# One split per pair of gate tiles, ordered a block ahead, and a shorter TensorE part of the sample sum

## The chip, the cores and the metric

The kernel runs on one core of one Trainium2 chip. Its time is the device time of that core in microseconds (us), taken as the median of several runs. The profile is one further execution, recorded by the hardware profiler; its engines are named PE (TensorE matmul), PEld (TensorE weight load), DVE (VectorE), ACT (ScalarE), POOL (GpSimd) and SP (SyncE, which issues most DMAs).

## The reference, cut to what matters

The model step has two layers, each a mixer (an RG-LRU in layer 0, a convolution in layer 1) followed by a PEER channel mixer. The change lies in the channel mixer alone. For every token it scores 2 x 128 keys per head, keeps 16 experts of 16,384 for each of 8 heads, and sums over them:

```python
top_s, pos = lax.top_k(cand, TOPK)
expert = jnp.take_along_axis(cand_idx, pos, axis=-1)
g = jax.nn.softmax(top_s, axis=-1)
u = u_tab[expert]
v = v_tab[expert]
act = jax.nn.gelu(jnp.einsum('td,thkd->thk', xb, u))
return jnp.einsum('thk,thkd->td', g * act, v)
```

There are 256 prompt tokens and 32 sample tokens. Both tables are 16,384 x 1024 in float32.

## The kernel before, in words

**Dense columns.** For 240 of the 256 prompt tokens nothing is gathered: the kernel computes the product with every expert. The tables are cut into 128 pieces of 128 experts each. Piece j of the first table gives a "u block": 24 matmuls (8 slices of the model dimension, each in three parts of a split product) into the tile `pu`, then a gelu by ACT into column j of `store`. A "gate phase" for each of three groups of pieces (0 to 45, 46 to 93, 94 to 127) multiplies `store` by the gates of the chosen experts: DVE builds one-hot tiles (`oA`, `oB`), PE multiplies them (`pgt`), DVE multiplies `store` by the result. Piece j of the second table gives a "v block": 24 matmuls (L1317 to L1319) that add to four accumulators `acc`.

**Split products.** A float32 matrix is split in two fp32r parts: ACT rounds it (the high part), DVE subtracts to get the low part, and three matmuls stand for one product. Each table tile `raw` is so split into `wh` (L234, ACT) and `wl` (L235, DVE), two blocks ahead of its use, into three buffers each. Columns j and j+1 of `store` are split together, as a pair, into `gh` (L439, ACT) and `gl` (L440, DVE), with two buffers each; `gw` holds which halves stand ready for which block. This is done by `wsplit(j)`, which does nothing if `gw` has j, or if the gate phase of j's group is still in the list `bg`.

**When a pair is split before the change.** An even block j calls `wsplit(j)`. After the block, `gw.pop(j)` removes only its own half. The odd block j+1 then calls `wsplit(j)` again: since the half of j has gone, the whole pair is split a second time into the other buffers, and block j+1 uses the halves of this second split. It then calls `wsplit(j + 2)` for the next pair. So there are two `gh` and two `gl` instructions a pair, both in front of the odd block.

**Order of blocks.** 82 u blocks come first, then two v blocks and two u blocks by turns until the u blocks end, then the remaining v blocks (the last two after the loop). Each engine executes its instructions in the order in which the program wrote them.

**The planner.** Beside the blocks runs background work on DVE: the gate phases (list `bg`), and the chain `bg2`. The latter holds the work for the 16 prompt tokens outside the dense columns (`extra`) and for the 32 sample tokens (`sample`). Both gather table rows by indirect DMAs from POOL into `grow` (L1369), multiply and sum on DVE. After each block, `pump` compares two estimates, `tp` for PE and `td` for DVE, and writes background steps into the program while `td` is lower. A `wsplit` that does something adds 620 to `td`.

**The sample sum.** The last part of `sample` adds 32 gathered rows of the second table, weighted by `act`. Its first `CPS[l]` steps are matmuls (`so`, L1485) that a copy by ACT brings to `sacc`; the others are DVE instructions into `sacd` (L1480 and L1478), one after each block. Each step orders the gather of the row two steps later.

Of the kernel before, what the change touches and what calls it, by code (L numbers as in the profile page):

```python
# [95 lines left out]
BG2 = (3, 0)  # L96
BG3 = (32, 32)
BG4 = 1
CPS = (14, 14)
J1 = 46  # L100
J2 = 94
CHUNKS = [(0, J1), (J1, J2), (J2, 128)]
# [99 lines left out]
class Stream:  # L202
# [39 lines left out]
    def next(self, src, idx, look=2):  # L242
        i = self.use_n
        self.use_n += 1
        assert self.items[i][0] is src and self.items[i][1] == idx, (i, self.items[i][1], idx)
        while self.split_n <= min(i + look, len(self.items) - 1):
            self._split()
        return self.hl.pop(i)


def peer_order():
    order = [("u", j) for j in range(RING)]
    u, v = RING, 0
    while v < 128:
        order += [("v", v), ("v", v + 1)]
        v += 2
        if u < 128:
            order += [("u", u), ("u", u + 1)]
            u += 2
    return order  # L260


class Kern:
# [867 lines left out]
    def peer(self, l):  # L1131
# [159 lines left out]
        gw = {}  # L1291

        def wsplit(j):
            c = [i for i, (j0, j1) in enumerate(CHUNKS) if j0 <= j < j1]
            if j in gw or not c or G[c[0]] in self.bg:
                return
            wh = wp.tile([128, 2, ND], F32R, name="gh", tag="gh", bufs=2)
            wl = wp.tile([128, 2, ND], F32R, name="gl", tag="gl", bufs=2)
            self.split_act(wh, wl, store[:, j % RING:j % RING + 2])
            self.td += 620  # L1300
            for i in range(2):
                gw[j + i] = (wh[:, i], wl[:, i])
# [8 lines left out]
        def vmm(j, w, d):  # L1311
            wh, wl = gw[j]
            vh, vl = w
            o = acc[d // 2][:, d % 2, :ND]
            f = j == 0 and d % 2 == 0
            e = j == 127 and d % 2 == 1
            nc.tensor.matmul(o, vh[:, d], wh, start=f, stop=False, skip_group_check=True)  # L1317
            nc.tensor.matmul(o, vh[:, d], wl, start=False, stop=False, skip_group_check=True)  # L1318
            nc.tensor.matmul(o, vl[:, d], wh, start=False, stop=e, skip_group_check=True)  # L1319

        for kind, j in peer_order():
            if kind == "v":
                if l == 0 and j in ADJ:
                    next(self.fg)
                for c, (j0, j1) in enumerate(CHUNKS):
                    if j == j0:
                        self.flush(G[c])
                wsplit(j - j % 2)
                if j % 2:
                    wsplit(j + 1)  # L1330
            if j >= 126 and kind == "v":
                continue
            w = self.wnext()
            if kind == "u":
                if j % 2 == 0:
                    pu = ps.tile([128, 2, NP], F32, name="pu", tag="mm", bufs=2)
                self.mm3(pu[:, j % 2, :ND], w, [(k, k) for k in range(KT)], aH, aL, 0, ND, True, True)
                if j % 2:
                    s = j % RING - 1
                    nc.scalar.activation(store[:, s:s + 2], pu[:, :, :ND], AF.Gelu)  # L1340
                done["u"] = self.udone = j + j % 2
                self.td += 1200
            else:
                if acc is None:
                    self.von = True
                    acc = [ps.tile([128, 2, NP], F32, name=f"acc{i}", tag="acc", bufs=4) for i in range(4)]
                for d in range(KT):
                    vmm(j, w, d)
                gw.pop(j)
                self.td += 1200  # L1350
            self.tp += 2690
            self.pump()
# [72 lines left out]
    def sample(self, l, TKs):  # L1425
# [15 lines left out]
        rows = {}  # L1441
        CP = CPS[l]
        gather = self.gatherer(ei, rows)
# [116 lines left out]
```

## Time and profile before

| | |
|---|---|
| median of 3 runs | 2409.42 us (2404.04 to 2414.55) |
| profiled execution | 2391.81 us, its span 2390.0 us |
| PE busy | 2100.3 us, 88% of the span |
| DVE busy | 1751.8 us, 73% |
| ACT busy | 977.2 us, 41% |
| POOL busy | 294.5 us, 12% |
| mean granted TensorE clock | 0.951 of full speed |
| DMA | 493.92 MB, mean 207 GB/s |

The u and v blocks of layer 0 lie between 258 and 1175 us, those of layer 1 between 1426 and 2360 us. A group of instructions reads: line, engine, operation, output and inputs, shape, count | busy time, mean ns of one | idle time of the engine just before them, and what ended it. A row of the table by stretches reads: stretch in us, its length, then busy time (and number of instructions) of each engine, the granted TensorE clock, the busy share of the DMA engines, and GB/s. In a timeline the columns are the start, the duration, the instruction, and in brackets the idle time before it and what ended it.

### The profile page before, as it was taken

Reading aid. Unit: us, or ns where it says so; the run is one execution under the profiler, and the core shown is the slowest. Engines: PE = TensorE matmul, PEld = TensorE weight load, DVE = VectorE, ACT = ScalarE, POOL = GpSimd, SP = SyncE. Lnnn points to the kernel's source line nnn. Section 1 sums busy time; section 2 is a strip of 40 time slices with the busy share of each in tenths; the row PEclk is TensorE's granted clock in tenths of the full one; section 3 lists DMA queues with packets and bytes.
Section 4 is the critical chain, followed back from the end, with each engine's and each line's share of the span. In section 5 each row is a group of like instructions: output and inputs, shape, how many; then the busy total and the mean of one; then the engine's idle time right before and its main releaser. Section 6 shows DMA issues by size and latency. Waiting matters only on the chain. (4 is left out here: it accounts for less than half of the span.)

```text
span 2390.0 us, 46892 instructions
## 1 busy us (share of the span) xinstructions
PE 2100.3 (88%) x19234; PEld 1944.3 (81%) x19234; DVE 1751.8 (73%) x3502; ACT 977.2 (41%) x1341; POOL 294.5 (12%) x329
## 2 busy tenths in 40 slices
PE   7999999988888888887888889999988888788877
PEld 3788999988888877776876689999888888778776
DVE  3877998887677766674776779898876777666666
ACT  1845444444333333343342544444443433333333
POOL 1100003030000000033112000120300000000330
PEclk9999999999999988998999999999998999899999
DMA  9774468576566544487579545685855666444873
GB/s 363 259 284 132 157 187 301 172 264 210 176 195 195 186 142 152 150 318 263 205 196 295 197 136 167 194 292 170 293 181 170 198 198 194 124 115 144 297 260 132
DMA packets 135912, 493.92 MB, mean 207 GB/s; under 512 B 16032, under 2 KB 16544, under 8 KB 135056
## 3 DMA queue, kind: packets, MB, share of 16 engines
q1 hardware_dynamic: 93168, 334.09, 43.3%
q0 software_dynamic: 42528, 156.83, 19.6%
q8 instruction: 151, 2.47, 0.4%
q14 instruction: 65, 0.53, 0.1%
HBM read 483.41 MB, written 7.39 MB: 205 GB/s over the span
## 5 line engine op out<-in xcount | busy, mean ns | idle before, releaser
L235 DVE TENSOR_TENSOR wl<-raw,wh 128x1024 fp32r<-128x1024 f32 x583 | 707.6, 1220 | 390.8 <-ACT wh L234 355.2
L234 ACT CAST wh<-raw 128x1024 fp32r<-128x1024 f32 x583 | 609.1, 1046 | 693.7 <-PE acc L1318 461.3
L1318 PE MATMUL acc<-gl,wh 128*128 128x240 f32 x2048 | 615.9, 301 | 200.9 <-DVE gl L440 200.6
L1318 PEld LDWEIGHTS acc<-gl,wh 128*128 128x128 f32 x2048 | 428.4, 209 | 223.6 <-DVE gl L440 223.6
L1317 PE MATMUL acc<-gh,wh 128*128 128x240 f32 x2048 | 606.0, 296 | 2.3 <-ACT gh L439 2.3
L1319 PE MATMUL acc<-gh,wl 128*128 128x240 f32 x2048 | 602.2, 294 | 0.0
L465 PE MATMUL pu<-aH,wl 128*128 128x240 f32 x2048 | 565.6, 276 | 9.2 <-DVE wl L235 9.1
L463 PE MATMUL pu<-aH,wh 128*128 128x240 f32 x2048 | 567.7, 277 | 0.0
L464 PE MATMUL pu<-aL,wh 128*128 128x240 f32 x2048 | 564.2, 276 | 0.0
L1317 PEld LDWEIGHTS acc<-gh,wh 128*128 128x128 f32 x2048 | 427.5, 209 | 18.1 <-issue 10.1
L1319 PEld LDWEIGHTS acc<-gh,wl 128*128 128x128 f32 x2048 | 429.0, 209 | 0.0
L465 PEld LDWEIGHTS pu<-aH,wl 128*128 128x128 f32 x2048 | 390.4, 191 | 11.5 <-DVE wl L235 11.5
L463 PEld LDWEIGHTS pu<-aH,wh 128*128 128x128 f32 x2048 | 389.0, 190 | 1.2 <-issue 0.8
L464 PEld LDWEIGHTS pu<-aL,wh 128*128 128x128 f32 x2048 | 389.5, 190 | 0.0
L439 ACT CAST gh<-store 128x480 fp32r<-128x480 f32 x254 | 150.3, 592 | 166.0 <-PE acc L1319 165.8
L440 DVE TENSOR_TENSOR gl<-store,gh 128x480 fp32r<-128x480 f32 x254 | 157.3, 651 | 23.5 <-ACT gh L439 23.4
L1340 ACT ACTIVATE store<-pu 128x480 f32<-128x480 f32 x128 | 73.1, 571 | 227.0 <-PE pu L465 226.9
L1369 POOL DMA_INDIRECT grow<-ur,ei x64 | 63.6, 994 | 752.2 <-DVE grow L1452 620.1
L463 PE MATMUL prj<-aH,wh 128*128 128x288 f32 x392 | 118.8, 303 | 0.0
L1282 DVE SCALAR_TENSOR_TENSOR store<-pgt,store 128x460 f32<-128x460 f32 (+3 forms) x184 | 83.8, 499 | 46.5 <-PE pgt L1275 46.1
L1251 DVE TENSOR_TENSOR oA<-c,iT 128x1280 f16<-128x1280 f16 (+1 forms) x136 | 116.4, 856 | 0.0
L464 PE MATMUL prj<-aL,wh 128*128 128x288 f32 x392 | 115.7, 295 | 0.0
(366 smaller groups left out, 2688.4 us busy)
## 6 DMA issues: line engine op xcount, KB each, us to landing
raw<-ut SPq DMA_DIRECT2D x256, 512.0 KB, 4.0
raw<-vt SPq DMA_DIRECT2D x256, 512.0 KB, 3.9
adaw<-wada POOLq DMA_DIRECT2D x56, 512.0 KB, 8.6
raw<-w SPq DMA_DIRECT2D x54, 512.0 KB, 5.4
raw<-wq SPq DMA_DIRECT2D x32, 512.0 KB, 3.6
adaw<-wada SPq DMA_DIRECT2D x18, 512.0 KB, 6.2
R<-us POOLq DMA_DIRECT2D x32, 286.5 KB, 10.0
store<-wada POOLq DMA_DIRECT2D x12, 512.0 KB, 4.2
```

Source lines behind the costliest of these rows:

```text
L234: nc.scalar.copy(hf, r)
L235: nc.vector.tensor_sub(lf, r, hf.bitcast(F32))
L439: self.nc.scalar.copy(h, src)
L440: self.nc.vector.tensor_sub(lo, src, h.bitcast(F32))
L463: nc.tensor.matmul(pt, h[:, kb], ah[:, ka, n0:n1], start=f, stop=False)
L464: nc.tensor.matmul(pt, h[:, kb], al[:, ka, n0:n1], start=False, stop=False)
L465: nc.tensor.matmul(pt, lo[:, kb], ah[:, ka, n0:n1], start=False, stop=e)
L1251: v.tensor_tensor(a, self.iota2[:, None].to_broadcast([128, g, 128, 2]), bc(0, 128), op=ALU.is_equal)
L1282: v.scalar_tensor_tensor(sv, pg[:, :n, q0 - j0:q1 - j0].rearrange("p t j -> p j t"), 1.0 / 4096.0, sv, op0=ALU.mult, op1=ALU.mult)
L1317: nc.tensor.matmul(o, vh[:, d], wh, start=f, stop=False, skip_group_check=True)
L1318: nc.tensor.matmul(o, vh[:, d], wl, start=False, stop=False, skip_group_check=True)
L1319: nc.tensor.matmul(o, vl[:, d], wh, start=False, stop=e, skip_group_check=True)
```

## The change

The two halves of a pair stay in `gw` until the odd block has used them, so that the pair is split once; the split of the next pair is ordered behind the matmuls of the even block, not in front of the odd block. `CPS` goes from (14, 14) to (8, 4): in layer 0 the first 8 and in layer 1 the first 4 steps of the sample sum are matmuls, the other 24 and 28 are DVE instructions. The number of dense columns stays at 240.

```diff
-CPS = (14, 14)
+CPS = (8, 4)
...
                 for d in range(KT):
                     vmm(j, w, d)
-                gw.pop(j)
+                if j % 2:
+                    del gw[j - 1], gw[j]
+                else:
+                    wsplit(j + 2)
                 self.td += 1200
             self.tp += 2690
             self.pump()
```

The lines behind L1349 move down by three (L1478 becomes L1481, L1485 becomes L1488).

On DVE, near the end of layer 1, where v blocks run alone and each is followed by one step of the sample sum, this stands in a row before (numbers tell buffers apart; `wl` belongs to a v block two blocks later):

```order
L1478 SCALAR_TENSOR_TENSOR sacd_26294<-grow_26521,sact_21230,sacd_26294 128x1024
L440 TENSOR_TENSOR gl_26599<-store_15315,gh_26598 128x480
L440 TENSOR_TENSOR gl_26603<-store_15315,gh_26602 128x480
L235 TENSOR_TENSOR wl_26609<-raw_26491,wh_26608 128x1024
L1478 SCALAR_TENSOR_TENSOR sacd_26294<-grow_26562,sact_21230,sacd_26294 128x1024
L235 TENSOR_TENSOR wl_26642<-raw_26532,wh_26641 128x1024
L1478 SCALAR_TENSOR_TENSOR sacd_26294<-grow_26595,sact_21230,sacd_26294 128x1024
```

and this with the change:

```order
L1481 SCALAR_TENSOR_TENSOR sacd_24956<-grow_25484,sact_20952,sacd_24956 128x1024
L235 TENSOR_TENSOR wl_25560<-raw_25454,wh_25559 128x1024
L440 TENSOR_TENSOR gl_25588<-store_15057,gh_25587 128x480
L1481 SCALAR_TENSOR_TENSOR sacd_24956<-grow_25521,sact_20952,sacd_24956 128x1024
L235 TENSOR_TENSOR wl_25597<-raw_25487,wh_25596 128x1024
L1481 SCALAR_TENSOR_TENSOR sacd_24956<-grow_25554,sact_20952,sacd_24956 128x1024
L235 TENSOR_TENSOR wl_25630<-raw_25524,wh_25629 128x1024
```

One `gl` a pair is left of two, and it stands behind the `wl` of the same even block and in front of that block's background step. Of the two `gl` before, the first is the second split of the pair in use.

On ACT, around the copy that ends the TensorE part of the sample sum in layer 1, before:

```order
L234 CAST wh_26227<-raw_26095 128x1024
L234 CAST wh_26265<-raw_26141 128x1024
L1471 COPY sacc_26293<-so_25964 128x512
L439 CAST gh_26302<-store_15315 128x480
L439 CAST gh_26306<-store_15315 128x480
L234 CAST wh_26312<-raw_26179 128x1024
L234 CAST wh_26345<-raw_26225 128x1024
L439 CAST gh_26376<-store_15315 128x480
```

and with the change:

```order
L234 CAST wh_24885<-raw_24767 128x1024
L234 CAST wh_24923<-raw_24802 128x1024
L439 CAST gh_24951<-store_15057 128x480
L1474 COPY sacc_24955<-so_24874 128x512
L234 CAST wh_24966<-raw_24840 128x1024
L234 CAST wh_24999<-raw_24883 128x1024
L439 CAST gh_25027<-store_15057 128x480
```

The `gh` of a pair stands behind the `wh` of the even block's call, a whole odd block ahead of its use. In the whole program the `gl` instructions fall from 254 to 128, and those of the sample sum on DVE rise from 36 to 52. On PE, `so` stands in 8 places a layer before, between v blocks; with the change in 4 places in layer 0 and 2 in layer 1, and 44 and 46 v blocks of the loop follow the last of them, where 20 followed before.

## The prediction

> **What bounds the kernel now.** I read the costliest groups first, then the waits, then the blocks in time, then the stages. The groups name one wait on PE, the busiest engine:
>
> ```profile
> L1318 PE MATMUL acc<-gl,wh 128*128 128x240 f32 x2048 | 615.9, 301 | 200.9 <-DVE gl L440 200.6
> L1319 PE MATMUL acc<-gh,wl 128*128 128x240 f32 x2048 | 602.2, 294 | 0.0
> L465 PE MATMUL pu<-aH,wl 128*128 128x240 f32 x2048 | 565.6, 276 | 9.2 <-DVE wl L235 9.1
> L440 DVE TENSOR_TENSOR gl<-store,gh 128x480 fp32r<-128x480 f32 x254 | 157.3, 651 | 23.5 <-ACT gh L439 23.4
> PE acc L1318 <- DVE gl L440: 200.6, 113, 5.5
> ```
>
> Of some 290 us in which PE stands idle, 200.6 are spent waiting for `gl`, 113 times, at most 5.5 us; the last row is from the list of waits (total, times, longest). The table's own low part `wl` costs the u blocks 9 us. The timeline of PE shows where it happens, here in layer 1:
>
> ```profile
> 2199.28 0.38 PE L1318 MATMUL acc<-gl,wh 128*128 128x240 f32 x1 [1.03 <-DVE gl L440]
> ...
> 2206.14 0.38 PE L1318 MATMUL acc<-gl,wh 128*128 128x240 f32 x1 [1.21 <-DVE gl L440]
> 2206.36 0.27 PE L1319 MATMUL acc<-gh,wl 128*128 128x240 f32 x1
> ...
> 2211.52 0.27 PE L1317 MATMUL acc<-gh,wh 128*128 128x240 f32 x1
> 2213.00 0.38 PE L1318 MATMUL acc<-gl,wh 128*128 128x240 f32 x1 [1.20 <-DVE gl L440]
> ```
>
> There is one wait per two blocks, 6.86 us apart. From 2206.36 to 2211.52 stand 46 steps of one matmul, 0.1122 us each, so a dense block of 24 takes 2.69 us and a pair 5.38. DVE meanwhile does this:
>
> ```profile
> 2301.38 1.28 DVE L1478 SCALAR_TENSOR_TENSOR sacd<-grow,sact,sacd 128x1024 f32<-128x1024 f32 x1
> ...
> 2308.29 1.28 DVE L1478 SCALAR_TENSOR_TENSOR sacd<-grow,sact,sacd 128x1024 f32<-128x1024 f32 x1
> 2309.49 1.22 DVE L440 TENSOR_TENSOR gl<-store,gh 128x480 fp32r<-128x480 f32 x2
> 2310.62 1.22 DVE L235 TENSOR_TENSOR wl<-raw,wh 128x1024 fp32r<-128x1024 f32 x1
> 2311.76 1.28 DVE L1478 SCALAR_TENSOR_TENSOR sacd<-grow,sact,sacd 128x1024 f32<-128x1024 f32 x1
> 2314.06 1.23 DVE L235 TENSOR_TENSOR wl<-raw,wh 128x1024 fp32r<-128x1024 f32 x1 [1.02 <-ACT wh L234]
> ```
>
> The two `gl` come behind the background step of the block before, and the odd block needs the first of them at once. DVE is not full: it sits idle 1.02 us a pair, waiting for a `wh` that itself waits until PE has freed a buffer. So the order of the work, not an amount of it, sets 6.86 us. From start to start a background step takes 1.20 us, a `wl` 1.14, a `gl` half of 1.13. The stages (columns: stretch, length, busy time of PE, PEld, DVE, ACT and POOL, clock, DMA share, GB/s):
>
> ```profile
> 258.00:504.00 246.00, 239.48 (x2521) 236.79 (x2519) 222.58 (x493) 111.76 (x140) 31.49 (x26) 1.00 0.65 210
> 504.40:1059.40 555.00, 469.40 (x4506) 458.53 (x4507) 390.99 (x580) 213.29 (x274) 57.65 (x60) 0.93 0.61 197
> 1059.40:1113.40 54.00, 43.38 (x273) 31.52 (x273) 19.75 (x22) 14.43 (x19) 21.27 (x18) 0.87 0.76 262
> 1113.40:1174.50 61.10, 50.97 (x435) 49.26 (x435) 49.60 (x51) 27.74 (x36) 12.86 (x13) 1.00 0.82 282
> 1689.00:2245.90 556.90, 470.61 (x4521) 459.68 (x4519) 393.34 (x583) 214.53 (x277) 52.91 (x50) 0.93 0.59 187
> 2245.90:2299.10 53.20, 42.45 (x273) 31.11 (x273) 19.82 (x22) 14.44 (x19) 19.64 (x17) 0.88 0.77 259
> 2299.10:2360.00 60.90, 51.47 (x434) 49.75 (x433) 49.72 (x51) 28.94 (x37) 12.87 (x13) 0.99 0.74 252
> ```
>
> The first is layer 0's u blocks alone. Then, a layer each: A, from the first v block to the sample sum; B, its TensorE part and what follows until DVE's first steps run; C, DVE's steps. In A the clock is 0.93, where the u blocks had 1.00: waits also bring half-speed stretches.
>
> **How much is lost there.** The same stages of layer 0 for `acc` in A, B and C, then for `pu` and `pgt` in A:
>
> ```profile
> 504.40:1059.40 555.00, 323.56 (x2376) 308.71 (x2376) 0.00 (x0) 0.93 0.61 197
> 1059.40:1113.40 54.00, 31.32 (x217) 29.75 (x217) 0.00 (x0) 0.87 0.76 262
> 1113.40:1174.50 61.10, 50.97 (x434) 49.21 (x433) 0.00 (x0) 1.00 0.82 282
> 504.40:1059.40 555.00, 129.55 (x1104) 127.21 (x1104) 13.16 (x23) 0.93 0.61 197
> 504.40:1059.40 555.00, 27.89 (x960) 27.78 (x68) 0.93 0.61 197
> ```
>
> A: (2376 + 1104) x 0.1122 = 390.5, with `pgt` 27.9 makes 418.4 dense; 555.0 leaves 136.6 us lost. Layer 1's A starts 0.7 of a block earlier, 420.3 dense, and loses 136.6 too. C: 18 blocks x 2.69 = 48.5, so 12.6 and 12.4 are lost. B: 9 blocks, 24.2, and eight places of `so` at 1.0 us (rows below): 54.0 - 32.2 = 21.8, and 21.0 in layer 1. Together 341 us in both layers.
>
> **The change part by part.** *The second split goes.* 126 `gl` and 126 `gh` fewer: 126 x 0.57 = 72 us of DVE's time and as many ACT casts. Neither engine is full, so this by itself is worth nothing; it matters as room. *The split moves.* A pair's `gh` is ordered behind the `wh` of the even block's call. That `wh` takes the buffer that the v block before freed; `gh` takes halves last read by the same v block. So it adds no wait on ACT; queued behind it there is the next `wh` or gelu, later by one cast of 0.59 us. `gl` stands directly behind a `wl` that belongs to the same coming block, so it is ready 0.57 us after something PE must have anyway, with a whole block in hand. What is late next is therefore `wl` or `wh`. The nearest rows for that are those of the u blocks alone, where the same two-block lead holds with DVE at 222.58 of 246 us: the whole kernel's wait there is the 9.2 us of L465. In A, DVE had 391 us; less 50 `gl` of 0.62 it has 360 against 418 of dense PE, 86%, less than the u blocks' 90%.
>
> Left over in A: below, 2 us a layer (the first pair has nothing ahead of it); above, 30, if the waits of DVE behind `pgt` and gathers are passed on to PE (the kernel's waits of DVE for `pgt` are 46 us). Since the u blocks with `pgt` lose almost nothing, I take 10, near the lower end. The planner now fills the freed 620 of each pair with earlier background work: the same steps, sooner, and A ends earlier for it. The gathers move with their steps. On POOL's queue they now meet other blocks' share of layer 0's twelve loads of weights into freed columns of `store`, which wait for `gl`:
>
> ```profile
> POOL store L387 <- DVE gl L440: 166.2, 8, 39.7
> ```
>
> These loads keep their blocks, and `gl` now comes earlier than they do, so a gather queued behind one waits no longer than before.
>
> *The sample sum.* The chain of waits and the groups give its prices:
>
> ```profile
> 2246.00 0.98 PE so L1485 x4
> 2253.73 0.99 PE so L1485 x8
> 2258.90 7.59 DMA grow<-vt,ei
> 2273.22 5.78 DMA grow<-vt,ei
> 2285.84 6.22 DMA grow<-vt,ei
> grow<-vt,ei POOLq DMA_INDIRECT x64, 5.6
> ```
>
> A place of `so` takes 1.0 us whether it holds one step or two. Places fall from 8 to 4 and 2: 10 us fewer. PE meets gathers (5.6 us from issue to landing, median) three times in layer 1's B, the last when DVE takes over. Fewer TensorE steps meet fewer: of 21.8 and 21.0 us lost I keep 14 and 10, since the handover and its slow clock stay; bounds 6 each and all of it.
>
> DVE gets 16 more steps, 24 and 28 in all, one after a block. Per block that is 1.20 + 1.14 + 0.28 = 2.62 us of DVE against 2.69 of PE: it fits, barely. The DMA engines are the other limit, since a block then loads 0.524 MB of table and 0.524 MB of gathered rows:
>
> ```profile
> 1113.40:1160.00 46.60, 37.79 (x322) 36.46 (x322) 39.23 (x41) 21.57 (x28) 12.86 (x13) 1.00 0.87 292
> 20.00:40.00 20.00, 16.40 (x61) 6.23 (x59) 5.45 (x26) 1.17 (x2) 3.18 (x6) 1.00 1.02 406
> ```
>
> At 3.43 us a block their share is 0.87, which full would be 2.98 us a block; at the 406 GB/s of the load at the start it would be 2.58. I take 2.85, between DVE's fit and the full share: 52 x 0.16 = 8 us over dense, bounds 0 and 52 x (3.43 - 2.69) = 38 (no gain). A gather has three steps' time, 8.1 us less 1.28, for its 5.6, so it need not stall DVE. The 18 to 20 blocks that follow have no background step and run dense.
>
> Sum, from the profiled 2391.8: A -273.2 + 20; B -42.8 + 24; C -25.0 + 8; `so` -10. That is 2092.8. The median of the runs lies 17.6 us above the profiled execution, so **2110**. Lower ends (4, 12, 0 for the 52 left over): 2074. Upper ends (60, 42.8, 38): 2199.
>
> **A rule on the clock.** The Trainium skill, "TensorE: Matmul & The Clock Gate", section "Why this matters for your kernels", asks for no idle gaps above some 3 us; shorter ones would leave the clock alone. Here waits of 1 to 3 us, with few up to 5.5, stand beside a clock of 0.93 over 555 us, so the trace does not bear the rule out as a threshold. By it much of the slow clock would have another cause and stay; the third rival prices that.
>
> **The rivals.**
> *DVE or the DMAs take over as the bound* (upper ends): for it, DVE's 2.62 of 2.69 and 1.05 MB a block; against it, the u blocks at 90% DVE. 2150 to 2200.
> *The wait only changes its name*: PE then waits for `wl` through the same chain, and a pair gains one `gl` of 0.57 us: 126 x 0.57 = 72, with 29 for the rest 2309. Against it, DVE's idle 1.02 us a pair waits for PE itself.
> *The slow clock stays*: 0.07 x 555 = 39 us a layer are not won back: 2110 + 78 = 2188. Against it, 1.00 over 246 us of u blocks.
> *Slower, through gathers.* Place: the DVE steps that read `grow`, 2 x 32 and 52. If blocks at full pace left each row's 5.6 us uncovered but for one block, a step would stall DVE 2.9 us: 116 x 2.9 = 336, 2446. It decides from 299 / 116 = 2.6 us a step. Against it:
>
> ```profile
> DVE grow L1407 <- DMA grow<-ur,xi: 18.4, 11, 6.1
> ```
>
> for 32 like steps, 0.6 us each. That the change doesn't do what it says is excluded by the order: 128 `gl` are left.
>
> **How the numbers follow.** Forecast 0.78 (own range 2074 to 2150); takeover 0.12; clock 0.04; renamed wait 0.03; gathers 0.02; no change 0.01. The range, 2060 to 2200, holds the first three, widened a little below because the 17.6 us between profile and median may differ. A measurement of this kernel tells about 0.5% from no change: faster 0.96, same 0.01, slower 0.03.
>
> **What would show it.** Right: L1318 without idle time before it but for the first pairs; odd blocks 2.69 us long like even ones; clock near 1.00 in A; DVE above 85% there; blocks with a `sacd` step at 2.7 to 3.0 us. Wrong: idle time before the third matmul of a block (now L1319) or before L1317, waiting for `wl` or `wh`; `wl` standing behind `sacd` steps that wait for `grow`; a clock below 0.95 without waits.

## The result, and the profile after

| | before | after |
|---|---|---|
| median of the runs | 2407.71 us (2404.04 to 2414.55, 4 runs) | 2091.29 us (2088.01 to 2104.38, 4 runs) |
| ratio to before, 95% interval | | 0.8693, 0.8651 to 0.8736 |
| profiled execution | 2391.81 us | 2090.24 us |
| its span, mean granted clock | 2390.0 us, 0.951 | 2088.4 us, 0.985 |

The change takes 316 us away, 13%. In the same order as the prediction, first the costliest groups of the changed kernel (line, engine, operation, shape, count | busy us, mean ns of one | idle time before, and what ended it; L1317 to L1319 keep their numbers, L1478 and L1485 are now L1481 and L1488):

```profile
L465 PE MATMUL pu<-aH,wl 128*128 128x240 f32 x2048 | 566.0, 276 | 9.7 <-DVE wl L235 9.3
L1318 PE MATMUL acc<-gl,wh 128*128 128x240 f32 x2048 | 567.4, 277 | 6.3 <-DVE gl L440 6.2
L1317 PE MATMUL acc<-gh,wh 128*128 128x240 f32 x2048 | 570.1, 278 | 2.3 <-ACT gh L439 2.3
L1319 PE MATMUL acc<-gh,wl 128*128 128x240 f32 x2048 | 566.5, 277 | 1.0 <-DVE wl L235 1.0
```

The idle time before L1318 falls from 200.9 to 6.3 us, and it does not turn up before the other two matmuls of a v block, where a wait that had only changed its name would stand. The matmuls themselves are shorter too: L1318 took 301 ns on average and now takes 277, because they no longer run at a lowered clock. In the list of waits (total, times, longest):

```profile
POOL store L387 <- DVE gl L440: 46.1, 4, 12.7
DVE sacd L1481 <- DMA grow<-vt,ei: 20.7, 19, 3.7
PE so L1488 <- DMA grow<-vt,ei: 6.8, 3, 2.6
PE acc L1318 <- DVE gl L440: 6.2, 8, 1.7
```

113 waits for `gl` have become 8. The timeline of PE, here the first and the last matmul of a pair of v blocks in stage A of layer 0:

```profile
704.62 0.28 PE L1317 MATMUL acc<-gh,wh 128*128 128x240 f32 x1
...
709.92 0.28 PE L1319 MATMUL acc<-gh,wl 128*128 128x240 f32 x1
```

48 matmuls start within 5.30 us, 0.113 us apart: the pair that took 6.86 us or more is dense. The stages, cut at the same events as before the change (stretch, length, busy time and number of instructions of PE, PEld, DVE, ACT and POOL, clock, DMA share, GB/s): A, B and C of layer 0, then of layer 1.

```profile
505.40:876.90 371.50, 367.46 (x4024) 364.78 (x4024) 329.05 (x501) 163.61 (x195) 73.17 (x56) 1.00 0.76 256
876.90:902.30 25.40, 20.85 (x130) 13.86 (x130) 7.33 (x8) 5.75 (x7) 12.24 (x10) 0.93 0.88 321
902.30:1023.40 121.10, 118.02 (x1036) 116.55 (x1034) 91.18 (x87) 55.47 (x64) 36.72 (x25) 1.00 0.86 307
1546.00:1917.60 371.60, 368.46 (x4026) 366.20 (x4027) 329.07 (x501) 163.58 (x195) 70.06 (x49) 1.00 0.74 247
1917.60:1931.10 13.50, 10.95 (x66) 6.92 (x66) 4.03 (x5) 3.17 (x4) 6.41 (x5) 0.87 0.89 311
1931.10:2056.60 125.50, 122.41 (x1082) 121.51 (x1081) 98.81 (x94) 59.43 (x68) 41.80 (x25) 1.00 0.82 289
```

C now holds also the v blocks that follow the last DVE step. In A the clock is 1.00 where it was 0.93, and DVE is busy 329 of 371.5 us, 89%. What A still loses is worked out as in the prediction, from the matmuls of `acc`, `pu` and `pgt` in layer 0's A:

```profile
505.40:876.90 371.50, 220.41 (x1896) 215.60 (x1896) 0.00 (x0) 1.00 0.76 256
505.40:876.90 371.50, 129.25 (x1104) 126.10 (x1104) 13.19 (x23) 1.00 0.76 256
505.40:876.90 371.50, 27.89 (x960) 27.61 (x68) 1.00 0.76 256
```

(1896 + 1104) x 0.1122 + 27.9 = 364.5 us are dense, so 7.0 us are lost, where 136.6 were; layer 1's A, with as many matmuls in 371.60 us, loses 7.1. B holds four whole blocks and four places of `so` in layer 0, 10.8 + 4.0 = 14.8 of its 25.4 us; in layer 1 two and two, 7.4 of 13.5. That leaves 10.6 and 6.1 us. Most of it is waiting for a gathered row that isn't there yet: the weight loads (PEld) of `so` wait 7.9 and 4.0 us for them. Layer 0's two long stalls, as the rows of PE have them:

```profile
885.78 1.05 PE L1488 MATMUL so<-grow,S 128*32 128x512 f32 x4 [2.52 <-DMA grow<-vt,ei]
896.90 1.05 PE L1488 MATMUL so<-grow,S 128*32 128x512 f32 x4 [1.76 <-DMA grow<-vt,ei]
```

In C, DVE works as the prediction's 2.62 us a block has it (layer 0):

```profile
917.55 1.28 DVE L1481 SCALAR_TENSOR_TENSOR sacd<-grow,sact,sacd 128x1024 f32<-128x1024 f32 x1
918.75 1.22 DVE L235 TENSOR_TENSOR wl<-raw,wh 128x1024 fp32r<-128x1024 f32 x1
919.89 0.65 DVE L440 TENSOR_TENSOR gl<-store,gh 128x480 fp32r<-128x480 f32 x1
920.46 1.28 DVE L1481 SCALAR_TENSOR_TENSOR sacd<-grow,sact,sacd 128x1024 f32<-128x1024 f32 x1
921.65 1.22 DVE L235 TENSOR_TENSOR wl<-raw,wh 128x1024 fp32r<-128x1024 f32 x1
923.40 1.28 DVE L1481 SCALAR_TENSOR_TENSOR sacd<-grow,sact,sacd 128x1024 f32<-128x1024 f32 x1 [0.53 <-DMA grow<-vt,ei]
```

One `gl` a pair stands between a `wl` and a step; the only idle time is a step's wait for its row. C has 43 blocks in layer 0 (115.7 us dense of 121.1) and 45 in layer 1 (121.1 of 125.5): 5.4 and 4.4 us lost, nearly all in the blocks beside DVE steps, which take 2.90 and 2.85 us on average (start to start, from the trace).

### The profile page after: what moved, and what is told of

The parts are those of the page before. It is cut to its first block, busy times and chain, and to the rows that moved or that the text cites. A ratio compares the mean times of both kernels' runs of the same rounds, so it can differ in the third digit from the quotient of the medians.

```text
span 2088.4 us, 46457 instructions
## 1 busy us (share of the span) xinstructions
PE 1987.2 (95%) x19170; PEld 1858.5 (89%) x19170; DVE 1690.8 (81%) x3392; ACT 915.4 (44%) x1215; POOL 360.5 (17%) x329
## 4 chain that ended last, share of the span: by engine, by line
PE 54%; issue 18%; DVE 12%; DMA 9%; POOL 4%; ACT 2%; SPq 0%; POOLq 0%; DVEq 0%; ACTq 0%
PE pu L465 7%; PE pu L463 7%; PE pu L464 7%; PE acc L1318 6%; PE acc L1317 6%; PE acc L1319 6%; DMA grow<-vt,ei 4%; POOL grow L1372 4%; DVE wl L235 3%; PE prj L463 2%; PE prj L465 2%; PE prj L464 2%; DMA R<-us 2%; PE adap L402 1%; PE pgt L1275 1%
## 5 line engine op out<-in xcount | busy, mean ns | idle before, releaser
L1318 PE MATMUL acc<-gl,wh 128*128 128x240 f32 x2048 | 567.4, 277 | 6.3 <-DVE gl L440 6.2
L1317 PE MATMUL acc<-gh,wh 128*128 128x240 f32 x2048 | 570.1, 278 | 2.3 <-ACT gh L439 2.3
L1319 PE MATMUL acc<-gh,wl 128*128 128x240 f32 x2048 | 566.5, 277 | 1.0 <-DVE wl L235 1.0
L1317 PEld LDWEIGHTS acc<-gh,wh 128*128 128x128 f32 x2048 | 391.0, 191 | 8.9 <-issue 4.6
L1318 PEld LDWEIGHTS acc<-gl,wh 128*128 128x128 f32 x2048 | 391.4, 191 | 8.5 <-DVE gl L440 8.3
L1319 PEld LDWEIGHTS acc<-gh,wl 128*128 128x128 f32 x2048 | 390.9, 191 | 1.7 <-DVE wl L235 1.6
L1372 POOL DMA_INDIRECT grow<-ur,ei x64 | 89.4, 1397 | 382.8 <-DVE grow L1455 275.2
L1372 POOL DMA_INDIRECT grow<-vt,ei x64 | 102.4, 1599 | 193.3 <-DVE grow L1455 113.2
L465 PE MATMUL prj<-aH,wl 128*128 128x288 f32 x392 | 116.1, 296 | 0.0
```

Of the source, the lines that this page charges most:

```text
L465: nc.tensor.matmul(pt, lo[:, kb], ah[:, ka, n0:n1], start=False, stop=e)
L1372: self.nc.gpsimd.indirect_dma_start(out=r, out_offset=None, in_=tab, in_offset=bass.IndirectOffsetOnAxis(ap=ei[:, w, c:c + 1], axis=0))
```

## The experiments

All ratios are to the kernel before, run on the same chip between the others, with 95% intervals. Times "in the places of `so`", of blocks and of stages are differences between starts in the profiled execution. The main explanation is the prediction's: the place of the split in DVE's order, in front of the block that needs it, set the time, and the sample sum added a little. Against it stand: that the two parts of the change need each other; that the amount of split work set the time; that ordering a block ahead, not splitting once, is what counts; and, for what is left in the blocks with a DVE step, that DVE's own work and not the gathers limits them.

### The split without the shorter TensorE part

```diff
-CPS = (8, 4)
+CPS = (14, 14)
```

> Both layers keep 14 TensorE steps of the sample sum; the pairs are split once and ahead, as in the change. Theory 1 (the second split stood right in front of its use, and that wait is nearly the whole gain): 2110 to 2130, that is 20 to 40 us above the change, since six and four places... of `so` more cost 10 us and the gathers that they meet cost 10 to 25. Theory 2 (the shorter TensorE part of the sample sum brings much of the gain): over 2200.

Measured: 2118.52 us (2115.57 to 2124.38), ratio 0.8800 (0.8767 to 0.8834). This edit alone brings some 291 us, and nearly all of the gain is the split's. In its waits, PE's stalls for gathered rows at `so` are longer than with the whole change (16.0 against 6.8 us), and `wl` waits behind `so`:

```profile
DVE wl L235 <- PE so L1488: 23.8, 5, 7.5
PE so L1488 <- DMA grow<-vt,ei: 16.0, 11, 2.5
PE acc L1318 <- DVE gl L440: 5.5, 7, 1.6
```

Its seven places of `so` a layer take 43.4 us together, the whole change's four and two 19.2: the difference of 24 us is about what the kernel is slower.

### The shorter TensorE part without the new split

```diff
-                if j % 2:
-                    del gw[j - 1], gw[j]
-                else:
-                    wsplit(j + 2)
+                gw.pop(j)
```

> 8 and 4 TensorE steps of the sample sum, but each pair is split twice at the old place. Theory 1: the pairs still cost about 6.9 us where background steps follow each block, so 2385 to 2410, at most 1% below before. Theory 2: 2300 or less.

Measured: 2388.52 us (2385.18 to 2390.39), ratio 0.9918 (0.9891 to 0.9944). It gains 21 us, so the two parts nearly add up: 291 + 21 = 313 of 316. The waits for `gl` are all there, and so is the lower clock over its v blocks of layer 0 (one row of the waits, then one of the stretches):

```profile
PE acc L1318 <- DVE gl L440: 204.7, 118, 3.7
```

```profile
505.00:1200.00 695.00, 584.12 (x5360) 555.80 (x5359) 489.42 (x712) 267.94 (x347) 90.80 (x92) 0.93 0.63 206
```

The places of `so` take 13.8 us in all against 34.8 before, 21 us less. That this is the whole gain isn't shown: the profiled execution is only 6.6 us shorter than the one before (2385.18 against 2391.81), because with the slow blocks the DVE steps reach the end of the v blocks, and layer 1's `pf`, the product that ends the layer, takes 16.5 us instead of 5.4, in part waiting for them:

```profile
PE pf L1505 <- DVE sacd L1478: 7.6, 2, 6.6
```

### Split once, but still in front of the odd block

```diff
                 if j % 2:
                     del gw[j - 1], gw[j]
-                else:
-                    wsplit(j + 2)
```

Without these lines the next pair is split by the odd block's own call: behind the even block's background step and in front of the odd block's matmuls, where the first split of a pair stood before the change.

> The change, but the split of the next pair stands in front of the odd block (where before had it) and not behind the even one; each pair is split once. Theory 1, in the form that only the second split of the pair in use was late: 2085 to 2105, as the change. In the other form, that the order a block ahead is needed as well: about 1 us of idle time a pair before L1318, 126 us, so 2180 to 2230.

Measured: 2108.61 us (2104.71 to 2112.12), ratio 0.8755 (0.8723 to 0.8787). This lies between the two ranges, much nearer to the first: 17 us over the change's median, 4 over the expected range. Splitting once gives nearly everything, because the pair in use is then never split again just before its odd block. Here too a pair is split an odd block ahead of its use; only the even block's background step now stands in front of the split. Having the split in front of that step is worth the rest, and its place is told by the trace:

```profile
PE acc L1318 <- DVE gl L440: 16.3, 15, 3.9
```

```profile
913.36 0.38 PE L1318 MATMUL acc<-gl,wh 128*128 128x240 f32 x1 [1.20 <-DVE gl L440]
```

That stall is in an even block beside a DVE step. DVE's rows just before it show how it comes about:

```profile
911.45 1.28 DVE L1479 SCALAR_TENSOR_TENSOR sacd<-grow,sact,sacd 128x1024 f32<-128x1024 f32 x1 [3.75 <-DMA grow<-vt,ei]
912.65 0.65 DVE L440 TENSOR_TENSOR gl<-store,gh 128x480 fp32r<-128x480 f32 x1
```

The step waits 3.75 us for its gathered row, and the `gl` behind it waits with it. Blocks are long beside such steps, in the first pair (5.61 us for its even block in layer 0, 3.83 with the change) and once soon after the u blocks end (5.49 and 6.97 us); the other v blocks of stage A take 2.7 to 3.1 us. So the place matters where DVE is nearly full, starts late, or has a step in front that waits for a gather.

### The change, with every split done twice

```diff
-                else:
+                elif j + 2 < 128 and j + 2 not in gw:
                     wsplit(j + 2)
+                    if j + 2 in gw:
+                        dh = wp.tile([128, 2, ND], F32R, name="dh", tag="dh", bufs=1)
+                        dl = wp.tile([128, 2, ND], F32R, name="dl", tag="dl", bufs=1)
+                        self.split_act(dh, dl, store[:, (j + 2) % RING:(j + 2) % RING + 2])
```

The second split goes into tiles that nobody reads; ACT and DVE do as much split work as before the change, at the new place.

> The change, and behind each split of a coming pair the same split once more, into tiles that nothing reads: ACT and DVE have as much to do as before (the planner counts one split). Theory 1 (order, not amount): the blocks of A stay dense, blocks with a sample step need 2.91 us of DVE, so 10 to 35 us above the change, 2100 to 2125. Theory 3 (amount: the 126 casts and subtractions themselves were the price): 2300 or more.

Measured: 2112.51 us (2105.89 to 2114.96), ratio 0.8776 (0.8746 to 0.8806). The whole second split, 72 us of DVE's time, costs 21 us when it stands a block ahead, against nearly 300 where it stood.

```profile
PE acc L1318 <- DVE gl L440: 8.7, 12, 2.1
```

This settles amount against order: what cost the time was that the odd block used halves split right in front of it, not that a second split was made. Where the 21 us lie is told in part only: 9 of them are in the blocks beside DVE steps, which take 3.11 and 2.99 us instead of 2.90 and 2.85, and of these layer 0's are no longer than in a repeat of the change (3.11 and 2.85, next).

### The change again, and two TensorE steps instead of 8 and 4

> The change itself, beside the next three on one chip: 2085 to 2100 by every theory.

Measured: 2095.37 us (2090.32 to 2097.92), ratio 0.8693 (0.8672 to 0.8713), as the first time. The blocks beside DVE steps take 3.11 and 2.85 us in its profiled execution.

```diff
-CPS = (8, 4)
+CPS = (2, 2)
```

> Two TensorE steps of the sample sum in each layer, 30 on DVE. Theory 1 (TensorE steps cost by the gathers that PE then waits for, DVE steps almost nothing as long as DVE keeps up): one place of `so` a layer, so 4 us of `so` and about 9 us of waits fewer, 8 DVE steps at 0.1 us more: 2075 to 2085. Theory 4 (DVE is full where its steps stand, so each further step costs): 2091 or more.

Measured: 2087.25 us (2081.75 to 2091.89), ratio 0.8663 (0.8642 to 0.8684). 8 us better than the change beside it and 2 us above the range expected by theory 1; the two intervals of the ratio overlap a little. The places of `so` fall to 4.1 us in all, 15 fewer, but 30 steps a layer are now beside blocks, which take 3.13 and 2.97 us there.

### No TensorE steps at all

```diff
-CPS = (8, 4)
+CPS = (0, 0)
```

With this the tiles `S2` and `so`, the copy to `sacc` and its product into the result `pf` go too; all 32 steps a layer are DVE's.

> No TensorE step of the sample sum: all 32 on DVE, without the tile of weights for PE and its part in the end of the layer. Theory 1: a few us less than with two steps, 2070 to 2083. Theory 4: 2091 or more.

Measured: 2071.12 us (2065.51 to 2074.74), ratio 0.8602 (0.8584 to 0.8620), and again in the next comparison:

> The kernel without TensorE steps, beside the next three on one chip: 2065 to 2080 by every theory.

2071.28 us (2066.35 to 2074.43), ratio 0.8614 (0.8588 to 0.8641). That beats the change by 24 us. 19 of these are the places of `so`. `pf` also ends sooner, 3.49 us against 5.84 and 5.28 in layers 0 and 1. The blocks beside the 32 steps take 2.92 and 2.81 us (2.98 and 2.87 in the repeat), about as long as with the change.

### The planner's old estimate

```diff
                 if j % 2:
                     del gw[j - 1], gw[j]
+                    self.td += 620
```

With the change the planner counts 620 less a pair for DVE and so writes background steps into the program earlier. Here it counts them again.

> The change, but the planner still adds 620 a second time for each pair, so that background work is written later, about where before had it. Theory 1 (PE is dense in A whatever DVE's room): 2085 to 2100, no difference from the change. Theory 5 (earlier background work is part of the gain, since the last DVE steps otherwise reach to the end of the v blocks): 2105 to 2125.

Measured: 2097.82 us (2094.61 to 2105.33), ratio 0.8713 (0.8690 to 0.8736). 2 us over the change beside it, which these intervals do not tell apart. Two effects of opposite sign hide in it. The stretches from the first v block to `pf` are 15 and 3 us shorter than in the repeat of the change beside it (6 and 2 us shorter than in its first profiled execution), but the DVE steps now reach the end of the v blocks, and `pf`, 7 and 12 us longer, waits for them:

```profile
PE pf L1509 <- DVE sacd L1482: 10.2, 2, 7.3
```

### No gathers for the DVE steps

```diff
-            if c + AH < 32:
+            if c + AH < CP:
                 gather(vrows, 1, c + AH)
-            r = rows.pop((1, c))
+            if c < CP:
+                r = rows.pop((1, c))
```

> The change, with the gathers of the rows for the DVE steps of the sample sum left out (24 and 28 rows; these steps all read the last row that TensorE used, so the sample sum is not the reference's). Theory 1 (blocks with such a step lose their last 0.1 us, and the handover its wait, to gathers that land late): 2080 to 2088, blocks with a step at 2.70 us. Theory 4 (DVE's own fill makes them longer): 2090 to 2098, blocks with a step as long as in the change.

Measured: 2086.80 us (2084.79 to 2092.75), ratio 0.8692 (0.8665 to 0.8720). By the time alone this could be no change: the ratio is the one of the change. The trace tells more. First the blocks beside steps of the change, layer 0 and layer 1, by stretches:

```profile
902.30:966.40 64.10, 61.05 (x530) 59.79 (x529) 56.22 (x53) 28.57 (x33) 36.72 (x25) 1.00 0.98 367
1931.10:2010.90 79.80, 76.71 (x675) 75.81 (x674) 72.18 (x68) 36.35 (x42) 41.80 (x25) 1.00 0.96 354
```

and the same of the kernel without gathers:

```profile
903.90:966.20 62.30, 62.30 (x557) 62.30 (x556) 59.44 (x58) 29.32 (x35) 2.66 (x5) 1.00 0.75 238
1927.90:1999.90 72.00, 72.00 (x644) 72.00 (x643) 67.98 (x64) 33.85 (x40) 0.00 (x0) 1.00 0.61 183
```

With the same DVE steps but no gathers PE has no idle time at all, at 94 to 95% of DVE busy, and a block takes 2.70 and 2.72 us. So DVE's 2.62 us do fit, and it is the gathers that lengthen these blocks (to 2.90 and 2.85 us, 3.11 and 2.85 in the repeat): with them the DMA engines are busy 96 to 98% of the time, at 354 to 367 GB/s. That alone does not tell whether the bytes set the length of a block or the delay of single gathers, and the next run leaves it open too.

### Without TensorE steps, with the DVE steps spread

```diff
-BG3 = (32, 32)
+BG3 = (24, 24)
```

`BG3` is the pace at which `pump` forces steps of the background chain once the gate phases are done: 24 forces one after three blocks of four. This and the next kernel are built on the one without TensorE steps.

> No TensorE steps, and background steps of the chain are forced after three blocks of four where the gate phases are over, not after each. If full blocks lose time (either theory), 2 to 6 us less than without: 2062 to 2075; if the steps then reach the end of the v blocks, 5 to 20 us more.

Measured: 2071.67 us (2064.80 to 2073.52), ratio 0.8618 (0.8591 to 0.8645): no difference from the unspread one (0.8614). The edit hardly did what it was meant to: the 32 steps lie over 34 blocks in each layer, where they lay over 32 and 33, since the planner still adds a step of its own whenever `td` is lower than `tp`; three of four would have been 43 blocks. So the run says little about spread steps. Layer 0's blocks there still take 2.95 us with the DMA share at 0.98, layer 1's 2.77.

### Without TensorE steps, without the wait for the last gate phase

```diff
-        self.idle2 = True
-        while len(self.bg) > 1:
-            yield 0
-        self.idle2 = False
```

> No TensorE steps, and the chain no longer waits for the last gate phase before the second half of the sample sum (it needs no accumulator of PE now). The steps stand earlier and end earlier: within 5 us of the kernel without, 2062 to 2080; slower only if steps and gate phase together overfill DVE.

Measured: 2066.18 us (2065.10 to 2074.64), ratio 0.8610 (0.8583 to 0.8637). It too is not told apart from the kernel without TensorE steps, and it could hardly differ: the first DVE step falls into the same v block of each layer, the 80th, with the wait and without, so the wait seems to have been over by then. Both beat the kernel before and the change; the fewest edits for that are `CPS = (0, 0)` and what goes with it.

## Why the prediction was right, step by step

**The bound.** It named one wait, PE for `gl` behind the background step, as caused by order and not by amount. The profile after has the wait gone without a successor, and the run with every split done twice a block ahead shows that it was order: the amount costs 21 us. The prediction gave the going of the second split no worth of its own and argued the gain from the place of the split. The run with one split in the old place divides it otherwise: that the second split is gone from in front of the odd block brings all but some 17 us of the gain, and the move only these. The sum did not need to tell the two apart.

**Terms of the sum**, from the profiled execution, in us for both layers:

| | lost before | predicted left | measured left |
|---|---|---|---|
| A | 273.2 | 20 | 14.1 |
| B | 42.8 | 24 | 16.7 |
| C | 25.0 | 8 | 9.8 |
| places of `so` | | -10 | -10 (16 places to 6) |

Measured, that is 2391.8 - 341.0 + 40.6 - 10 = 2081.4; the profiled execution took 2090.2. 8.0 of the missing 8.8 us lie outside the v stages, where the change does nothing: the way to layer 0's first v block took 505.4 us (504.4 before), from layer 0's `pf` to layer 1's first v block 522.7 (517.5), from there to the end 31.8 (30.0). Other runs of the same part differ as much: 514.7 to 524.4 us for the middle stretch in these kernels. That the predicted 2092.8 is so near to 2090.2 is partly luck: A and B gave 13 us more than predicted, and C and the parts outside took 11 of them back. Nor can terms of this size be checked on one execution: in the repeat of the change layer 0 takes 526.7 us from its first v block to `pf`, in the execution read here 517.9.

**A** was priced near the lower end, by the u blocks' rows, and came out lower still. What is left there in layer 0 is the first pair's wait for `gl` (0.77 us; its 1.14 us for `gh` lie just in front of A, with the change and before), the matmuls of `hfp`, which belong to the background work and which the dense sum doesn't count (3.56 us), and one long u block (5.35 us, 6.33 in layer 1) just before the u blocks end. In that block DVE's wait for a gathered row is passed on to PE, as the upper end for A had it; DVE's row, then PE's:

```profile
766.79 1.23 DVE L1455 SCALAR_TENSOR_TENSOR grow<-grow,hft 128x1024 f32<-128x1024 f32 x1 [3.53 <-DMA grow<-ur,ei]
769.22 0.38 PE L465 MATMUL pu<-aH,wl 128*128 128x240 f32 x1 [2.39 <-DVE wl L235]
```

The `wl` that PE needs stands behind that step on DVE. It happens once a layer, and so costs 2.7 and 3.6 us and not 30.

**B** was the least certain term. I kept the stall at the handover and its slow clock; the gathers' stalls stayed, at 2.52 and 1.76 us in layer 0 and 2.55 in layer 1, and so did the clock (0.93 and 0.87), but at the handover PE has no gap: the last block of B takes 4.41 and 3.54 us through the clock alone. So 16.7 us are left and not 24.

**C**: blocks with a step at 2.85 us were predicted, 2.90 and 2.85 measured, and the row of 0.87 of the DMA engines' time at 3.43 us a block, which gave 2.98 for full engines, was the nearer of the two rows. The 2.58 us from the load at the start was not reached.

**The step that failed**, though the range held, is the last one of the sum: "The median of the runs lies 17.6 us above the profiled execution". That offset was the one profiled execution's own, which at 2391.81 us lies below all timed runs of the kernel before (2394.66 to 2414.55). Nothing of it carried over: the median of the changed kernel lies 1.0 us above its profiled execution, and the other kernels' profiled executions lie within 7 us of their medians. (Each of those executions is itself one of the runs of its median; 2391.81 is none of the runs of the kernel before.) Without this term the forecast would have been 2093 and not 2110 us. Why that one execution was shorter isn't settled by any run here.

**The rivals.** The wait with a new name (2309) falls with L1317 and L1319, which have 2.3 and 1.0 us of idle time. The slow clock that stays (2188) falls with 1.00 in A. The gathers that make it slower (2446, deciding from 2.6 us a step) cost 20.7 us in 19 waits, over 50 steps 0.4 us each. The takeover by DVE and the DMA engines (2150 to 2200) is true in small: in the blocks beside steps the DMA engines are full, but this costs 0.2 us a block and not 0.7.

## What to carry to other kernels

A wait of one engine for another that is only 73% busy can be a question of order, as it was here: look at what stands directly in front of the awaited instruction in its engine's queue, and whether it has to be made there at all. Here the awaited split was a repeat; once it was gone, little was left for the order to gain (17 us). Then move what is awaited in front of steps that can themselves wait, for a gathered row for instance. Such waits are paid twice where they also lower the clock, so the gain can exceed the idle time that the profile names (291 us here by the split alone, for 200.6). In layer 0's stage A before, PE waited 85.5 us for `gl`, 48 times, and the clock of 0.93 over 555 us took by estimate another 39 (0.07 x 555): some 124 of the 136.6 us that were lost there. One profiled execution is compared with another profiled execution; the distance from there to a median of runs is not a constant of the chip.

## What the runs showed of the hardware

**In the kernel before, the clock mostly fell after an idle gap of 2 to 3 us.** In its profile, a gap of 2.28 us is followed by a stretch of half speed. The row of PE's timeline, then the stretches around it:

```profile
829.64 0.57 PE L1318 MATMUL acc<-gl,wh 128*128 128x240 f32 x1 [2.28 <-DVE gl L440]
```

```profile
814.40:819.00 4.60, 2.99 (x26) 2.80 (x25) 4.60 (x6) 1.54 (x2) 0.00 (x0) 1.00 0.43 127
829.40:832.80 3.40, 3.16 (x15) 3.17 (x16) 1.89 (x3) 0.00 (x0) 0.00 (x0) 0.52 0.51 154
832.80:836.20 3.40, 3.40 (x32) 3.40 (x32) 1.28 (x2) 1.05 (x1) 0.00 (x0) 1.00 0.36 128
```

The first of these has a gap of 1.61 us and keeps the clock; behind the gap of 2.28 us it is 0.52 for one stretch of 3.4 us, and 1.00 again after it. Counted over the profiled execution of the kernel before: of 89 gaps of 0.5 to 1.5 us of PE, 4 were followed by such a stretch, of 22 gaps of 1.5 to 2 us 6, of 33 gaps of 2 to 3 us 29, and of 8 of 3 to 3.5 us all. With the sample sum alone changed it was 6 of 94, 6 of 22, 27 of 31, and 9 of 10. Stretches of half speed fall from 52 to 12 with the change. The Trainium skill, "TensorE: Matmul & The Clock Gate", section "Why this matters for your kernels", warns of idle gaps above some 3 us; in these two kernels gaps of 2 to 3 us were followed by half speed nine times in ten. It is no fixed rule: with the change it was 1 of 3, and in all twelve profiled executions without the old split, this one included, 26 of 44. Why some gaps of that length leave the clock alone isn't shown here. The 1.2 us gap a pair in layer 1's C before left the clock at 0.99, and the 2 to 3 us gaps of A cost more than they lasted.

**Half gathered, half contiguous, the DMA engines were 96 to 100% busy at 354 to 387 GB/s** (the highest in the change's layer 0, below). The load of contiguous pieces at the kernel's start had 406 at a share of 1.02.

```profile
937.30:966.40 29.10, 26.05 (x218) 24.79 (x218) 24.50 (x24) 11.92 (x14) 16.76 (x13) 1.00 1.00 387
```
